# Mixer A's values in two passes, with the sums of the exponentials added up beside them

## The chip, the cores and the metric

The kernel runs on one core of a Trainium2 chip. The metric is the device time of one execution in microseconds. The engines are named as in the profile: PE is TensorE (PEld its weight loads), DVE is VectorE, ACT is ScalarE, POOL is GpSimd, SP issues DMAs.

## The reference

One layer of a hybrid diffusion backbone. 1024 latent tokens and 128 prompt tokens, each 1024 wide, are normed and modulated, projected to queries, keys, values and gates of two mixers (8 heads of 64 over 2 key groups each), attended, gated with SiLU, and projected back. Mixer A attends to all 1024 latent keys and 128 cached ones, mixer B to a window and the cached ones with a sink logit:

```python
def global_attn_latent(q, k_lat, v_lat, k_ctx, v_ctx):      # mixer A
    k_all = jnp.concatenate([k_ctx, k_lat], axis=1)
    v_all = jnp.concatenate([v_ctx, v_lat], axis=1)
    def one_block(qblk):                                    # 128 queries
        s = jnp.einsum('bqkgd,bskd->bkgqs', qblk, k_all).astype(jnp.float32) * (d ** -0.5)
        p = jax.nn.softmax(s, axis=-1).astype(v_all.dtype)
        return jnp.einsum('bkgqs,bskd->bqkgd', p, v_all)
...
def merge_out(o_a, g_a, o_b, g_b, w_out):
    return jnp.concatenate([o_a * jax.nn.silu(g_a), o_b * jax.nn.silu(g_b)], axis=-1) @ w_out
...
xs = xs + gate * merge_out(o_a, g_a, o_b, g_b, w_out[l])
```

All inputs are float32. The outputs are both token sets and the prompt's new keys and values.

## The kernel before

TensorE takes its operands in a rounded 32-bit form (`F32R`). To keep float32 accuracy each operand is kept as a high part (the rounded value) and a low part (what the rounding left), and a product is summed from two or three passes: high x high, and the two mixed ones. Weights, hidden states, keys, values, probabilities (`ph`, `pl`) and gated outputs (`ogh`, `ogl`) are split in this way.

The first 300 us project gates, queries, keys and values. The rest is the attention loop. It goes over `units` (t, m, g): t is a tile of 128 tokens (1 to 8 latent, then 0 the prompt), g the key group with four query heads, m the mixer (0 is A, 1 is B). For a latent t the order is A, B of group 0, A, B of group 1. A unit of mixer A has nine blocks of 128 keys, one of mixer B three or four, a prompt unit one. Each block is a slot of the loop; `tick()` opens a slot and runs what `later(n, f)` put on the agenda n slots before. In each slot the loop issues `scores` for its block, then what is `due`, then some items of the output projection of an earlier tile (2.5 on average), then `values` for the block of three slots before (`LAG`). `in_order` fixes the order of the instructions on each engine to the order in which they are written.

For a block of mixer A, `scores` makes two passes into a PSUM bank "B" (keys by four heads' 128 queries, 512 columns), ScalarE takes the exponential (`pe`), ScalarE rounds it (`ph`), and GpSimd (VectorE for b in `PL_DVE`) subtracts to get `pl`. The maximum that is subtracted in the exponent was found before: `max_items` multiplies the queries with all keys in twelve pieces of 384 columns (`pmx`, bank "A") and VectorE reduces each to its row maximum (`mx`); this is done for the mixer A unit two ahead, spread over slots by `MX_AT`. A later small transposition (`ptm`, also "A") puts the maxima into the queries' low tile `qb`.

`values` accumulates into a bank "C" (`pv`), with 128 rows. The weights `two` are 64 columns of the values' high part beside 64 columns that are 1 for mixer A, and the values' low part for mixer B. So for mixer A rows 64 to 127 hold the sum of the exponentials:

```python
nc.tensor.matmul(pv, two, ph, ...)                  # L1141
if m == 0: nc.tensor.matmul(pv[0:64, :], vl, ph, ...)   # L1143
nc.tensor.matmul(pv, two, pl, ...)                  # L1144
```

After the last block, on the agenda by `END_AT`: `inverse` (for mixer A, ScalarE takes the logarithm of the sums and the exponential of its negative; for B it copies the lower half), `gated` (VectorE multiplies, or adds for B, and GpSimd multiplies with the gate tile `sgl`), `parts` (the split into `ogh`, `ogl`). Once both mixers of a group are done, `out_items` puts 24 passes of the output projection in the queue `outq`. When a tile's projection is complete, VectorE multiplies with the adaLN gate (L1218) and adds the residual (L1219).

Mixer B's softmax works from the other side: `weight_items` computes scores with queries in rows (`sn`, bank "A", slots 0 to 3 of the mixer A unit before), VectorE adds the mask and takes the minimum of the negatives (L942), ScalarE takes the exponential with its sum (L928), and `scores` transposes the result; VectorE makes `pl` from PSUM (L1117). Its inverse sums reach the gate tile through a small DMA, and GpSimd multiplies them into `sgl` (L986).

PSUM has two banks each of "A", "B" and "C", and one each of "D" and "E". `pe` has three buffers (`PES`), `ph` and `pl` four.

Of the kernel before, what the change touches and what calls it, by code (L numbers as in the profile page):

```python
# [9 lines left out]
F32 = mybir.dt.float32  # L10
# [8 lines left out]
P = 128  # L19
D = 1024  # L20
KT = D // P
HD = 64
# [12 lines left out]
KS = (0, 1, 4, 5, 2, 3, 6, 7)  # L35
PL_DVE = (4,)
LAG = 3
# [23 lines left out]
OUTRATE = 2.5  # L61
PADRATE = 3
POOL_LO = ("gb",)
NOG = 5
PES = 3
# [43 lines left out]
def hybrid_step(ctx, tc, x_prompt, x_sample, cache_k_a, cache_v_a, cache_k_b, cache_v_b,  # L109
# [17 lines left out]
    def later(n, f):  # L127

        agenda.setdefault(now[0] + n, []).append(f)
# [577 lines left out]
    v_hi = kv.tile([P, 2, 20, 2, HD], F32R, name="v_hi")  # L707
    v_lo = kv.tile([P, 20, HD], F32R, name="v_lo")

# [369 lines left out]
    ogp = ctx.enter_context(tc.tile_pool(name="ogp", bufs=NOG, side="right"))  # L1079
    w2 = ctx.enter_context(tc.tile_pool(name="w2", bufs=2, side="right"))  # L1080
    def blocks(t, m, g):

        if t == 0:
            k = (khp[:, g, :], klp[0:68, g, :]) if m == 0 else 0
            return [(k, v_hi[:, m, 18 + g], v_lo[:, 18 + g, :])]
        if m == 0:
            return [((kha[:, g, b, :], kla[:, g, b, :]), v_hi[:, 0, 2 * b + g], v_lo[:, 2 * b + g, :]) for b in range(9)]
        p0, p1_ = window(t)
        at = {p: b + 1 for b, p in enumerate(POS)}
        return [(p - p0, v_hi[:, 1, 2 * at.get(p, 0) + g], None) for p in range(p0, p1_)]  # L1090

# [15 lines left out]
    def scores(i, b, blk):  # L1107
# [20 lines left out]
        if b in PL_DVE:  # L1128
            later(1, lambda: nc.vector.tensor_tensor(pl, pe, ph, op=ALU.subtract))
        else:  # L1130
            nc.gpsimd.tensor_tensor(pl, pe, ph, op=ALU.subtract)  # L1131
        return ph, pl

    def values(i, b, last, blk, ph, pl):
        t, m, g = units[i]
        _, vh, vl = blk
        if b == 0:
# [3 lines left out]
        nc.tensor.matmul(pv, two, ph, start=(b == 0), stop=False)  # L1141
        if m == 0:
            nc.tensor.matmul(pv[0:64, :], vl, ph, start=False, stop=False)  # L1143
        nc.tensor.matmul(pv, two, pl, start=False, stop=last)  # L1144
# [5 lines left out]
        def inverse():  # L1150
            v["rs"] = w2.tile([64, 512], F32, tag="rs", name=f"rs{i}", bufs=1)
            if m == 1:
                nc.scalar.copy(v["rs"], pv[64:128, :])
                return
            nc.scalar.activation(v["rs"], pv[64:128, :], AF.Ln)
            nc.scalar.activation(v["rs"], v["rs"], AF.Exp, scale=-1.0)

        def gated():
# [8 lines left out]
            nc.gpsimd.tensor_tensor(of, of, sgl.pop(i), op=ALU.mult)  # L1167
            later(GATE_LATE, lambda: load_gate(i + 2))
            v["of"] = of

# [175 lines left out]
```

## Time and profile before

| | |
|---|---|
| runs | 714.02, 711.7, 713.01; median 713.01 us |
| the profiled execution | 711.52 us, of which the span is 709.6 |
| PE busy | 691.6 us, 97% of the span |
| PEld busy | 558.5 us, 79% |
| DVE busy | 469.3 us, 66% |
| ACT busy | 409.9 us, 58% |
| POOL busy | 334.2 us, 47% |

Busy is the time in which an engine has at least one instruction in work; idle time is given with the instruction that ended it and what it had waited for (the releaser). A group is all instructions of one line, engine and form, with count, summed duration and mean. A matmul's end is modelled, so successive matmuls overlap in the records.

### The profile page before, as it was taken

To read this page: it belongs to the slowest core of one execution; us is meant where nothing else is said; L and a number is where in the kernel's file an instruction comes from. 1 tells how busy PE (TensorE), PEld (TensorE's weight loads), DVE (VectorE), ACT (ScalarE), POOL (GpSimd) and SP (SyncE) were. 2 spreads that over 40 slices of the span, in tenths; PEclk is the share of its full clock that TensorE was granted. 3 is DMA by queue.
4 is the path that set the end of the run, shared out by engine and by line. 5 is a ranking of instruction groups with operands and counts; after the bars stand their busy time and mean duration, and the time that the engine had idled before them with its cause. 6 is when DMAs were issued, how large, how long until landed. Compare 5 with 4: busy or idle time off the path is not lost. (4 is left out here: it accounts for less than half of the span.)

```text
span 709.6 us, 10604 instructions
## 1 busy us (share of the span) xinstructions
PE 691.6 (97%) x3508; PEld 558.5 (79%) x3508; DVE 469.3 (66%) x1019; ACT 409.9 (58%) x829; POOL 334.2 (47%) x356
## 2 busy tenths in 40 slices
PE   7999999999999999989999999999999999999987
PEld 4778988878787889966788888888888888787865
DVE  4667257967848945647867578666775776675662
ACT  5646412412403431188777887787778777877760
POOL 3547023233213421256756655665576557555660
PEclk9999999999999999999999999999999999999999
DMA  8962283358353116332222121212221221222323
GB/s 316 415 211 102 78 302 74 90 154 263 84 139 104 37 39 215 123 108 57 78 68 85 50 82 53 71 57 75 68 82 38 79 71 50 78 72 70 104 67 121
DMA packets 53560, 78.58 MB, mean 111 GB/s; under 512 B 7096, under 2 KB 25720, under 8 KB 52608
## 3 DMA queue, kind: packets, MB, share of 16 engines
q1 hardware_dynamic: 45328, 65.96, 28.1%
q10 hardware_dynamic: 8176, 11.94, 6.3%
q8 instruction: 28, 0.46, 0.3%
q14 instruction: 28, 0.23, 0.1%
HBM read 58.69 MB, written 19.18 MB: 110 GB/s over the span
## 5 line engine op out<-in xcount | busy, mean ns | idle before, releaser
L1131 POOL TENSOR_TENSOR pl<-pe,ph 128x512 fp32r<-128x512 f32 x130 | 167.7, 1292 | 145.0 <-DVE nm L942 67.5
L882 DVE TENSOR_REDUCE mx<-pmx 128x1 f32<-128x384 f32 x192 | 101.4, 552 | 56.3 <-PE pmx L881 54.8
L1123 ACT ACTIVATE pe<-st 128x512 f32<-128x512 f32 x146 | 86.8, 594 | 28.2 <-PE st L1121 27.4
L1127 ACT CAST ph<-pe 128x512 fp32r<-128x512 f32 x146 | 90.6, 621 | 4.8
L1141 PE MATMUL pv<-ph,v_hi 128*128 128x512 f32 x208 | 82.8, 398 | 2.2 <-DVE spare L1165 2.2
L1144 PE MATMUL pv<-pl,v_hi 128*128 128x512 f32 x208 | 82.4, 396 | 0.0
L1212 PE MATMUL po<-wo,ogh 128*128 128x512 f32 x216 | 72.6, 395 | 0.2 <-DVE yt L1219 0.2
L174 POOL TENSOR_TENSOR rs_q<-ms_q,mhalf 128x8 f32<-128x8 f32 x18 | 34.1, 1896 | 80.9 <-DVE ms_q L172 80.9
L942 DVE CUSTOM_DVE_ANT_0 sn<-sn,mask,nsink 128x512 f32<-128x512 f32 (+1 forms) x64 | 46.4, 724 | 38.0 <-PE sn L939 37.6
L881 PE MATMUL pmx<-kha,qt 128*128 128x384 f32 x192 | 61.2, 363 | 0.4 <-ACT pen L928 0.2
L1120 PE MATMUL st<-qt,kha 128*128 128x512 f32 x144 | 58.2, 404 | 1.9 <-ACT pe L1123 1.1
L1121 PE MATMUL st<-qb,kla 68*128 68x512 f32 x144 | 57.5, 399 | 1.1 <-DVE qb L901 1.1
L1143 PE MATMUL pv<-ph,v_lo 128*64 128x512 f32 x146 | 57.6, 395 | 0.0
L1144 PEld LDWEIGHTS pv<-pl,v_hi 128*128 128x128 f32 x208 | 39.2, 189 | 16.4
L928 ACT ACTIVATE pen<-sn,nm 128x512 f32<-128x512 f32 (+2 forms) x72 | 45.0, 626 | 6.5 <-DVE nm L942 3.1
L1116 ACT CAST ph<-st 128x512 fp32r<-128x512 f32 x62 | 36.4, 587 | 19.9 <-PE st L1115 18.7
L1141 PEld LDWEIGHTS pv<-ph,v_hi 128*128 128x128 f32 x208 | 39.3, 189 | 10.6 <-ACT ogh L1177 2.4
L646 ACT CAST qo0q<-ptq 128x512 fp32r<-128x512 f32 x18 | 10.6, 586 | 60.7 <-PE ptq L643 55.8
L1212 PEld LDWEIGHTS po<-wo,ogh 128*128 128x128 f32 x216 | 40.0, 188 | 6.8 <-DVE yt L1219 0.6
L1117 DVE TENSOR_TENSOR pl<-st,ph 128x512 fp32r<-128x512 f32 x62 | 42.5, 686 | 2.7 <-ACT ph L1116 2.1
L1212 PE MATMUL po<-wo,ogl 128*128 128x512 f32 x108 | 42.6, 394 | 0.0
L881 PEld LDWEIGHTS pmx<-kha,qt 128*128 128x128 f32 x192 | 35.6, 191 | 6.4 <-DVE mx L882 1.3
(213 smaller groups left out, 1699.2 us busy)
## 6 DMA issues: line engine op xcount, KB each, us to landing
qt<-qd SPq DMA_DIRECT2D x36, 256.0 KB, 3.0
wm<-in_w_mod_ss_dram SPq DMA_DIRECT2D x7, 1024.0 KB, 10.0
qd<-qo0q ACTq DMA_DIRECT2D x36, 128.0 KB, 2.4
qd<-qo1q ACTq DMA_DIRECT2D x36, 128.0 KB, 2.4
sgl<-gd SPq DMA_DIRECT2D x36, 128.0 KB, 2.2
out_dram<-yt SPq DMA_DIRECT2D x17, 256.0 KB, 2.0
xn<-in_x_sample_dram SPq DMA_DIRECT2D x8, 512.0 KB, 7.2
wg<-in_w_mod_g_dram SPq DMA_DIRECT2D x4, 1024.0 KB, 8.3
```

What stands on the lines that cost most here:

```text
L881: nc.tensor.matmul(pm[:, 0:384], lhs, kha[:, g, 3 * b : 3 * b + 3, :], start=True, stop=True)
L882: nc.vector.tensor_reduce(mx[:, h, b : b + 1], pm[:, 0:384], axis=AX.X, op=ALU.max)
L942: nc.vector.tensor_tensor_reduce(s, s, mask[:, m0 : m0 + n], -1.0, nsink[:, 4 * g + h : 4 * g + h + 1], op0=ALU.add, op1=ALU.min, accum_ou ...
L1120: nc.tensor.matmul(s, kh, qtile[i], start=True, stop=False)
L1121: nc.tensor.matmul(s, kl, qbtile[i], start=False, stop=True)
L1123: nc.scalar.activation(pe, s, AF.Exp)
L1127: nc.scalar.copy(ph, pe)
L1131: nc.gpsimd.tensor_tensor(pl, pe, ph, op=ALU.subtract)
L1141: nc.tensor.matmul(pv, two, ph, start=(b == 0), stop=False)
L1143: nc.tensor.matmul(pv[0:64, :], vl, ph, start=False, stop=False)
L1144: nc.tensor.matmul(pv, two, pl, start=False, stop=last)
L1212: nc.tensor.matmul(po[n], a, wo_parts[KT * n + k][lo], start=(k == KS[0] and p == 0), stop=(k == KS[-1] and p == 2))
```

## The change

For mixer A the values' low part moves into the columns that held ones, as for mixer B, and the pass with `v_lo` goes: `pv` gets high and low products in its two halves from two passes for each block. The sum of the exponentials is made in another way. In a latent unit the nine `pe` are added up in one tile `acc`, by GpSimd for b = 1 to 3 and by VectorE for b = 4 to 8, one slot after the block; `acc` is split into a high part (ScalarE) and a low part (GpSimd) two and three slots after the last addition, and two passes with ones as weights sum both over the keys into a bank "A" five slots after it. A prompt unit, which has one block, passes its `ph` and `pl` to the same two passes. ScalarE takes logarithm and exponential of 256 columns in the layout of the gate tile, GpSimd multiplies the result into `sgl`, and `gated` adds the two halves as for mixer B. `PL_DVE` goes from b = 4 to b = 1, 2, 3; `NOG`, the buffers of `ogh` and `ogl`, from 5 to 4.

```diff
-PL_DVE = (4,)
+PL_DVE = (1, 2, 3)
+SUMS_AT = (2, 3, 5)
+ADDED = 4
-NOG = 5
+NOG = 4
@@ split_values
-        nc.vector.tensor_tensor(v_lo[:, j : j + 2, :], src[:, 0], v_hi[:, 0, j : j + 2, 0, :], op=ALU.subtract)
-        nc.vector.tensor_tensor(v_hi[:, 1, j : j + 2, 1, :], src[:, 1], v_hi[:, 1, j : j + 2, 0, :], op=ALU.subtract)
+        nc.vector.tensor_tensor(v_hi[:, :, j : j + 2, 1, :], src, v_hi[:, :, j : j + 2, 0, :], op=ALU.subtract)
...
-        for b in range(0, 20, 4):
-            later(4 + b // 2, lambda b=b: nc.gpsimd.tensor_scalar(
-                v_hi[:, 0, b : b + 4, 1, :], gain4, 0.0, 1.0, op0=ALU.mult, op1=ALU.add))
+        later(4, lambda: nc.gpsimd.tensor_scalar(ones_v, gain4[:, 0, :], 0.0, 1.0, op0=ALU.mult, op1=ALU.add))
@@ scores
+        if t == 0:
+            later(5, lambda: row_sums(i, ph, pl))
+        else:
+            later(1, lambda: add_up(i, b, pe))
         return ph, pl
+
+    adding, scaling = {}, {}
+
+    def add_up(i, b, pe):
+        if b:
+            (nc.vector if b >= ADDED else nc.gpsimd).tensor_tensor(acc, adding.pop(i), pe, op=ALU.add)
+        adding[i] = acc if b else pe
+        if b < 8:
+            return
+        hi, lo = acc_parts
+        for n, f in zip(SUMS_AT, (lambda: nc.scalar.copy(hi, acc),
+                                  lambda: nc.gpsimd.tensor_tensor(lo, acc, hi, op=ALU.subtract),
+                                  lambda: row_sums(i, hi, lo))):
+            later(n, f)
+
+    def row_sums(i, *parts):
+        ss = bank("A", f"ss{i}")
+        for j, a in enumerate(parts):
+            nc.tensor.matmul(ss[0:HD], ones_v, a, start=(j == 0), stop=(j == 1))
+        iv = w2.tile([P, 2 * P], F32, tag="iv", name=f"iv{i}", bufs=1)
+
+        def inverse():
+            for s in range(2):
+                h = slice(HD * s, HD * s + HD)
+                nc.scalar.activation(iv[h].rearrange("p (c n) -> p c n", c=2),
+                                     ss[0:HD].rearrange("p (c s n) -> p s c n", s=2, n=P)[:, s], AF.Ln)
+            nc.scalar.activation(iv, iv, AF.Exp, scale=-1.0)
+            scaling[i] = iv.rearrange("p (c n) -> p c n", c=2)
+
+        if units[i][0]:
+            later(1, inverse)
+        else:
+            inverse()
@@ values
-        if m == 0:
-            nc.tensor.matmul(pv[0:64, :], vl, ph, start=False, stop=False)
         nc.tensor.matmul(pv, two, pl, start=False, stop=last)
...
-            if m == 1:
-                nc.scalar.copy(v["rs"], pv[64:128, :])
-                return
-            nc.scalar.activation(v["rs"], pv[64:128, :], AF.Ln)
-            nc.scalar.activation(v["rs"], v["rs"], AF.Exp, scale=-1.0)
+            nc.scalar.copy(v["rs"], pv[64:128, :])
...
-                                        op=ALU.add if m else ALU.mult)
-            nc.gpsimd.tensor_tensor(of, of, sgl.pop(i), op=ALU.mult)
+                                        op=ALU.add)
+            v["of"] = of
+            if t and m == 0:
+                later(1, gate_on)
+            else:
+                gate_on()
+
+        def gate_on():
+            if m == 0:
+                nc.gpsimd.tensor_tensor(sgl[i], sgl[i], scaling.pop(i), op=ALU.mult)
+            nc.gpsimd.tensor_tensor(v["of"], v["of"], sgl.pop(i), op=ALU.mult)
             later(GATE_LATE, lambda: load_gate(i + 2))
```

More of the change, by code (lines that the diff above doesn't have):

```diff
@@ L707, in hybrid_step @@
     v_hi = kv.tile([P, 2, 20, 2, HD], F32R, name="v_hi")
-    v_lo = kv.tile([P, 20, HD], F32R, name="v_lo")
+    ones_v = kv.tile([P, HD], F32R, name="ones_v")
     POS = [0, 2, 3, 5, 6, 8, 9, 11]
@@ L1080, in hybrid_step @@
     w2 = ctx.enter_context(tc.tile_pool(name="w2", bufs=2, side="right"))
+    acc = w2.tile([P, 512], F32, name="acc", bufs=1)
+    acc_parts = [w2.tile([P, 512], F32R, name=f"acc{n}", bufs=1) for n in ("h", "l")]
     def blocks(t, m, g):
@@ L1084, in blocks @@
             k = (khp[:, g, :], klp[0:68, g, :]) if m == 0 else 0
-            return [(k, v_hi[:, m, 18 + g], v_lo[:, 18 + g, :])]
+            return [(k, v_hi[:, m, 18 + g])]
         if m == 0:
-            return [((kha[:, g, b, :], kla[:, g, b, :]), v_hi[:, 0, 2 * b + g], v_lo[:, 2 * b + g, :]) for b in range(9)]
+            return [((kha[:, g, b, :], kla[:, g, b, :]), v_hi[:, 0, 2 * b + g]) for b in range(9)]
         p0, p1_ = window(t)
         at = {p: b + 1 for b, p in enumerate(POS)}
-        return [(p - p0, v_hi[:, 1, 2 * at.get(p, 0) + g], None) for p in range(p0, p1_)]
+        return [(p - p0, v_hi[:, 1, 2 * at.get(p, 0) + g]) for p in range(p0, p1_)]
     pvb, og = {}, {}
```

3 lines of the change are left out of this document (1 added, 2 removed).

## The prediction, made before the change was run

> **What bounds the kernel now.** I read the page first (busy shares, the 40 slices, the costliest groups), then busy time by stage, then the order of time of single engines inside one stretch of attention, then the waits.
>
> ```profile
> span 709.6 us, 10604 instructions
> PE 691.6 (97%) x3508; PEld 558.5 (79%) x3508; DVE 469.3 (66%) x1019; ACT 409.9 (58%) x829; POOL 334.2 (47%) x356
> L1131 POOL TENSOR_TENSOR pl<-pe,ph 128x512 fp32r<-128x512 f32 x130 | 167.7, 1292 | 145.0 <-DVE nm L942 67.5
> L1143 PE MATMUL pv<-ph,v_lo 128*64 128x512 f32 x146 | 57.6, 395 | 0.0
> ...
> 320.00:350.00 30.00, 27.73 (x125) 20.60 (x124) 23.79 (x52) 24.70 (x52) 20.75 (x21) 1.00 0.26 75
> 350.00:650.00 300.00, 300.00 (x1450) 241.66 (x1449) 204.69 (x437) 235.17 (x466) 180.06 (x193) 1.00 0.21 65
> ```
>
> The columns of the last two rows are the stretch, its length, then PE, PEld, DVE, ACT and POOL busy, the clock, the DMA share. From 350 to 650 us TensorE never stops (300.00 of 300), at a granted clock of 1.00; VectorE has 68%, ScalarE 78%, GpSimd 60%. So the attention loop is bound by TensorE, and a matmul taken out is worth its pitch, as long as the other engines keep up with a shorter loop. The pitch isn't the 395 ns of the group, since matmuls overlap; it is read from starts:
>
> ```profile
> 493.90 0.40 PE L1141 MATMUL pv<-ph,v_hi 128*128 128x512 f32 x1
> 494.13 0.40 PE L1143 MATMUL pv<-ph,v_lo 128*64 128x512 f32 x1
> 494.37 0.40 PE L1144 MATMUL pv<-pl,v_hi 128*128 128x512 f32 x1
> ...
> 439.85 0.76 DVE L942 CUSTOM_DVE_ANT_0 sn<-sn,mask,nsink 128x512 f32<-128x512 f32 x1 [0.23 <-PE sn L939]
> 463.74 0.76 DVE L942 CUSTOM_DVE_ANT_0 sn<-sn,mask,nsink 128x512 f32<-128x512 f32 x1 [0.24 <-PE sn L939]
> 487.58 0.76 DVE L942 CUSTOM_DVE_ANT_0 sn<-sn,mask,nsink 128x512 f32<-128x512 f32 x1 [0.22 <-PE sn L939]
> ```
>
> 494.37 less 493.90 is two pitches: 0.235 us each. The other three rows are the first mixer B score of three successive pairs of units (one of mixer A with nine key blocks, one of mixer B with about four): the loop turns once in (487.58 - 439.85) / 2 = 23.86 us. Over 300 us that is 12.57 pairs, so a pair holds 204.69 / 12.57 = 16.3 us of VectorE, 18.7 of ScalarE and 14.3 of GpSimd.
>
> **The change part by part, for one pair.**
>
> TensorE: nine `v_lo` passes go, two passes with ones come: -7 x 0.235 = -1.64, leaving 22.2 us. (A prompt unit of mixer A loses one and gains two.) If all of it counted, 16 pairs would give 26 us. The cover over the other engines shrinks by as much.
>
> VectorE: before, one subtraction of the nine `pl` is on it (b = 4); now three are, and five additions (b = 4 to 8). All read two operands in SBUF, as L1129 does. Price by starts:
>
> ```profile
> 473.58 0.69 DVE L1129 TENSOR_TENSOR pl<-pe,ph 128x512 fp32r<-128x512 f32 x1 [1.45 <-ACT ph L1127]
> 474.19 0.55 DVE L882 TENSOR_REDUCE mx<-pmx 128x1 f32<-128x384 f32 x1
> 335.83 3.78 POOL L1131 TENSOR_TENSOR pl<-pe,ph 128x512 fp32r<-128x512 f32 x3
> ```
>
> The next starts 0.61 after L1129: +7 x 0.61 = 4.3, so VectorE works 16.3 + 4.3 = 20.6 us in a pair.
>
> GpSimd: two `pl` less, three additions (b = 1 to 3), the subtraction for the low part of the sum, and one product with the inverse sums. Three in 3.78 us with ends overlapped are 1.25 each; the product is a 128x256 one, some 0.7:
>
> ```profile
> L1167 POOL TENSOR_TENSOR spare<-spare,sgl 128x256 f32<-128x256 f32 x26 | 19.2, 738 | 0.5
> 484.77 0.59 ACT L1155 ACTIVATE rs<-pv 64x512 f32<-64x512 f32 x1 [0.86 <-PE pv L1144]
> 485.39 0.63 ACT L1156 ACTIVATE rs<-rs 64x512 f32<-64x512 f32 x1
> L1177 ACT CAST ogh<-spare 128x256 fp32r<-128x256 f32 x36 | 14.4, 402 | 1.5 <-POOL spare L1167 1.5
> ```
>
> +2 x 1.25 + 0.7 = 3.2, so 17.5 us. ScalarE: the logarithm and exponential on 512 columns go (0.62 + 0.63); in come a plain copy (0.6), the high part of the sum (0.6), and three passes over 256 columns, each near L1177's 0.40: 2.4 - 1.25 = +1.15, 19.9 us. On sums alone every engine still fits under 22.2.
>
> What the sums leave out is that VectorE and GpSimd get in each other's way. The rows that show it lie where `w_out` and the last gate weights are split:
>
> ```profile
> 344.65 1.33 POOL L1131 TENSOR_TENSOR pl<-pe,ph 128x512 fp32r<-128x512 f32 x1 [1.34 <-ACT ph L1127]
> 344.87 1.67 DVE L1038 TENSOR_TENSOR wo_big<-wraw,wo_big 128x512 fp32r<-128x512 f32 x1
> L236 DVE TENSOR_TENSOR wlogb<-rawgb,whigb x4: 691/726/1772, 243.5 to 249.4; 128x512 fp32r<-128x512 f32 x4
> L236 POOL TENSOR_TENSOR wlogb<-rawgb,whigb x4: 1287/1586/1736, 244.4 to 250.1; 128x512 fp32r<-128x512 f32 x4
> L1129 DVE TENSOR_TENSOR pl<-pe,ph x16: 691/693/700, 313.3 to 661.3; 128x512 fp32r<-128x512 f32 x16
> ```
>
> (The last three give shortest / median / longest in ns.) The subtraction at 344.87 takes 1.67 instead of 0.69: GpSimd's subtraction runs until 345.98, and VectorE ends 0.56 after that. It waited 0.98. In L236, where both engines do such subtractions at once, both stretch: 1772 against 691, 1736 against 1287. VectorE's operations with a PSUM operand show no such spread. L1129, the very form that is added eight times, shows none either: 691 to 700 in all 16, because at b = 4 GpSimd waits just then. So the price of a meeting is bounded by 0 (L1129) and 0.98 (L1038). For eight operations in a pair that is 0 to 7.8 us. I take the chance of meeting: GpSimd busy 17.5 of 23.9 = 0.73, the rest of a running operation on average 0.55 (half of 1.25, less for the short ones): 8 x 0.73 x 0.55 = 3.2 us. That is 0.4 for each, just under the middle of the two rows: the additions for b = 4 to 8 are issued in the slots in which GpSimd does five `pl` in a row, unlike L1129's.
>
> The Trainium skill, page "SBUF — State Buffer", section "SBUF: two separate sides", says that one pair of SBUF ports is shared, that a VectorE operation with two SBUF inputs and a GpSimd operation that reads SBUF take it as an exclusive lock, and that the later "fully blocks". L1129's 16 rows alone would say that this form is free of it, and the sum would be rival 1's; by the page each meeting costs all that is left of the other's operation, and the sum is the one below. L1038 and L236 agree with the page.
>
> Waits: VectorE now idles 7.6 us in a pair; the parts of it:
>
> ```profile
> DVE mx L882 <- PE pmx L881: 40.9, 41, 1.5
> DVE sn L942 <- PE sn L939: 34.3, 48, 1.3
> DVE pl L1129 <- ACT ph L1127: 20.3, 14, 2.1
> ```
>
> Over the 15 pairs of this stretch the wait for mixer B's scores is 34.3 / 15 = 2.3 each. These lie in slots 0 to 3, where a score matmul waits for its bank and for TensorE's turn, and don't vanish with more work behind them; the two `pl` for b = 1 and 2 now fall between them and may fill 1.2. I take 1.7, between 1.1 and 2.3. The other waits I let vanish, since VectorE will be late there.
>
> So a pair takes 20.6 + 3.2 + 1.7 = 25.5 us on VectorE, against 22.2 on TensorE: +1.6. How that reaches TensorE: VectorE runs in order, so an addition that waits for GpSimd holds back the row maxima and mixer B's `pl` behind it. The maxima's products, scores, transposes and now the sums share two PSUM banks ("A"); a product can't start until the reduction two before it has read its bank. TensorE stalls there, in slots 5 to 12. In slots 1 and 2 `ss` takes a turn in these banks as well: the next score waits for the logarithms, which stand ahead of the score's exponential on ScalarE. ScalarE is dense there, so `pe` of b = 2 to 4 comes some 1.1 us later, and additions with it; I count that in the 1.7. A `pe` buffer (three) is now held until its addition: two slots of slack, free. The gate loads are issued a slot later on SP, which idles; NOG 4 instead of 5 isn't reached in the steady pairs. The ones and the value splits are in a stage where TensorE is busy without a gap; free.
>
> The sum: 13 steady pairs and the two of t = 1. In the latter TensorE has gaps already (27.73 of 30), so its saving counts for little; I take the same +1.6. 15 x 1.6 = 24.0. In the last pair (t = 8, second group) no nine-block unit follows, the twelve maxima are absent, VectorE is free and TensorE's saving counts: -1.6. The prompt units: two matmuls more (0.5) against two shorter inverses (-0.6 each) where TensorE waits for the bank `pv`: 0. Together +22.4. The profiled execution took 711.52: 733.9. The median of the runs, 713.01, is 1.5 above it: 735.5 us.
>
> **The rivals.**
>
> 1. Additions fall into GpSimd's gaps, as L1129 does: no port cost. VectorE has 20.6 + 1.7 = 22.3, level with TensorE, and order decides:
>
> ```profile
> 455.35 1.02 DVE L882 TENSOR_REDUCE mx<-pmx 128x1 f32<-128x384 f32 x2 [0.96 <-PE pmx L881]
> 477.23 1.02 DVE L882 TENSOR_REDUCE mx<-pmx 128x1 f32<-128x384 f32 x2 [1.27 <-PE pmx L881]
> 478.17 0.69 DVE L1218 TENSOR_TENSOR po<-po,wo_big 128x512 f32<-128x512 f32 x1
> 484.83 0.68 DVE L901 TENSOR_TENSOR qb<-ptm,diag 4x512 fp32r<-4x512 f32 x1 [0.36 <-PE ptm L900]
> ```
>
> In every second pair the output's two operations stand at 478.17, and VectorE has no gap from 477.23 until 0.36 before 484.83. Two additions (1.22) less 0.36 and some 0.3 of slack make this pair 0.55 longer. The other has gaps (0.96 before 455.35) and gains about 0.75 of TensorE's 1.64. 7 x 0.55 - 6 x 0.75 - 1.6 = -2.3: 710.7 us. Against it: GpSimd's added work goes into those gaps.
>
> 2. TensorE stays the bound, VectorE keeps up: 146 passes less 36 is 110 x 0.235 = 25.9: 687 us. For it: the sums of busy time, all under 22.2. Against it: VectorE would have to run at 93% in order without one wait that TensorE feels. It is the other side: it decides from a port cost under 0.5 us in a pair, if the waits for scores close too.
>
> 3. GpSimd never idles when VectorE asks: each of eight waits L1038's 0.98, 7.8 in a pair, while the waits for scores vanish: 28.4, +4.5 x 15 - 1.6 = +66: 779 us. For it: five `pl` in a row behind the three additions. Against it: GpSimd's 17.5 leave it idle a quarter of the time.
>
> **How the numbers follow.** The forecast has 0.64, with a range of its own from 710 to 760 (a port cost of two thirds to four thirds of 3.2, waits of 1.1 to 2.3: -0.1 to +3.3 in a pair). Rival 1 has 0.13, rival 2 0.13, rival 3 0.10. 0.3% (2.1 us) is about what a measurement here can tell from no change. Faster: rival 2 and 0.05 of rival 1, 0.18. Same: 0.05 of rival 1 and 0.02 of the forecast, 0.07. Slower: 0.75. The range of 8 in 10 leaves out rival 2 below and most of rival 3 above: 706 to 758.
>
> **What would show it.** Right: the `pl` on VectorE and the additions with means well over 0.69 and longest near 1.9; GpSimd's `pl` longer than 1.29; TensorE under 95% busy between 350 and 650, its idle time before `pmx`, put down to VectorE's reductions; a pair of 25 to 26 us by the starts of `sn`. `ss` should start without a wait. Wrong: additions at a flat 0.69 (no port cost), or TensorE still at 300 of 300 with pairs of 22.2.

## The result, and the profile after

The changed kernel takes 766.58 us (median of four runs, 766.33 to 769.15) against 712.49 (711.7 to 714.02) before: a ratio of 1.0764, 95% interval 1.0734 to 1.0795. The forecast was 735.5 us, range 706 to 758. The direction is right, the loss is more than twice as large: 54 us instead of 22. The profiled execution took 769.15 us, with a span of 767.4.

The page of the changed kernel: span, engines, and the groups that the prediction named; the last line is `pmx` before the change.

```profile
span 767.4 us, 10712 instructions
PE 707.7 (92%) x3398; PEld 549.5 (72%) x3398; DVE 583.6 (76%) x1121; ACT 425.2 (55%) x881; POOL 423.8 (55%) x402
L1132 POOL TENSOR_TENSOR pl<-pe,ph 128x512 fp32r<-128x512 f32 x98 | 141.4, 1455 | 86.2 <-ACT ph L1128 76.6
L880 PE MATMUL pmx<-kha,qt 128*128 128x384 f32 x192 | 76.3, 414 | 30.3 <-DVE mx L881 28.1
L1143 DVE TENSOR_TENSOR acc<-acc,pe 128x512 f32<-128x512 f32 x80 | 88.2, 1103 | 5.4 <-ACT pe L1124 2.0
L1130 DVE TENSOR_TENSOR pl<-pe,ph 128x512 fp32r<-128x512 f32 x48 | 50.8, 1059 | 15.2 <-ACT ph L1128 14.7
L1143 POOL TENSOR_TENSOR acc<-acc,pe 128x512 f32<-128x512 f32 x32 | 44.6, 1392 | 5.7 <-PE st L1122 4.5
...
L881 PE MATMUL pmx<-kha,qt 128*128 128x384 f32 x192 | 61.2, 363 | 0.4 <-ACT pen L928 0.2
```

110 matmuls went, as planned, and TensorE still shows 16 us more busy time: the records of `pmx`, where it stalls most, went from a mean of 363 ns to 414, and at times the granted clock is lower (below). The additions and subtractions on VectorE take 1103 and 1059 ns instead of 690, GpSimd's subtraction 1455 instead of 1292. TensorE's idle time ahead of `pmx` went from 0.4 us to 30.3, nearly all put down to VectorE's reductions.

Busy time by stretch (length, PE, PEld, DVE, ACT, POOL, clock, DMA share), and what VectorE itself waited for in the same stretch (total, times, longest):

```profile
350.00:700.00 350.00, 320.98 (x1407) 238.67 (x1407) 304.53 (x549) 255.26 (x522) 258.74 (x238) 0.98 0.19 59
...
DVE sn L941 <- ACT pe L1124: 19.2, 11, 1.7
DVE pl L1130 <- ACT ph L1128: 10.4, 13, 1.1
DVE sn L941 <- PE sn L938: 6.2, 15, 1.6
```

The pairs by the starts of `qb`, once a pair: twelve steady pairs lie between the two rows of each kernel (its third and its fifteenth `qb`), before and after.

```profile
341.99 0.68 DVE L901 TENSOR_TENSOR qb<-ptm,diag 4x512 fp32r<-4x512 f32 x1
628.03 0.68 DVE L901 TENSOR_TENSOR qb<-ptm,diag 4x512 fp32r<-4x512 f32 x1 [0.36 <-PE ptm L900]
...
353.12 0.68 DVE L900 TENSOR_TENSOR qb<-ptm,diag 4x512 fp32r<-4x512 f32 x1
675.84 0.68 DVE L900 TENSOR_TENSOR qb<-ptm,diag 4x512 fp32r<-4x512 f32 x1
```

A pair took 286.04 / 12 = 23.84 us and takes 322.72 / 12 = 26.89. Over the 13 pairs of the 350 us, VectorE works 304.53 / 13 = 23.4 us in each and idles 3.5; TensorE is busy for 92% of the time, no longer for all of it.

Where the 57.8 us of span came from, by the starts of `qb`. The first `qb` is made ahead of the loop, so the table begins with the second:

| part | before | after | change | predicted |
|---|---|---|---|---|
| before the second `qb` | 303.4 | 306.0 | +2.7 | 0 |
| first two pairs | 38.6 | 47.1 | +8.5 | +3.2 |
| twelve steady pairs | 286.0 | 322.7 | +36.7 | +19.2 |
| last three stretches between `qb` | 48.7 | 53.2 | +4.5 | 0 |
| after the last `qb` | 32.9 | 38.3 | +5.4 | 0 |

The first row is spread between executions: other kernels below with the same code up to there reach the second `qb` at 302.4 to 306.0, and the median run is 2.6 us shorter than the profiled one. In the prediction's sum one more pair with +1.6 and the last with -1.6 make the 0 of the fourth row.

How an addition loses its time, in order of time of VectorE, GpSimd and the products for the maxima:

```profile
474.26 0.68 DVE L1143 TENSOR_TENSOR acc<-acc,pe 128x512 f32<-128x512 f32 x1
474.74 1.36 POOL L1132 TENSOR_TENSOR pl<-pe,ph 128x512 fp32r<-128x512 f32 x1 [1.42 <-ACT ph L1128]
476.66 2.53 DVE L1143 TENSOR_TENSOR acc<-acc,pe 128x512 f32<-128x512 f32 x2
476.90 1.74 POOL L1132 TENSOR_TENSOR pl<-pe,ph 128x512 fp32r<-128x512 f32 x1
478.60 1.18 POOL L1208 TENSOR_TENSOR spare<-spare,sgl 128x256 f32<-128x256 f32 x1
479.11 1.01 DVE L881 TENSOR_REDUCE mx<-pmx 128x1 f32<-128x384 f32 x2
479.71 0.19 PEld L880 LDWEIGHTS pmx<-kha,qt 128*128 128x128 f32 x1 [0.53 <-DVE mx L881]
```

The addition at 474.26 meets an idle GpSimd until nearly its end and takes 0.68. The two at 476.66 take 2.53 instead of 1.30 (0.61 to the next start and 0.69), among GpSimd's subtraction (1.74 instead of 1.29) and gate product (1.18 instead of 0.73). The two reductions of maxima stand behind them and start at 479.11; the next product of TensorE waits 0.53 for its bank. This is the path that the prediction described.

In every second pair an output tile's two operations stand on VectorE as well, and the stall is longer. The addition behind them, the product that waits, and the windows behind the stall, in two such pairs:

```profile
400.73 1.58 DVE L1143 TENSOR_TENSOR acc<-acc,pe 128x512 f32<-128x512 f32 x1
402.83 0.44 PE L880 MATMUL pmx<-kha,qt 128*128 128x384 f32 x1 [1.96 <-DVE mx L881]
404.00:407.00 3.00, 3.00 (x12) 2.62 (x11) 2.41 (x7) 1.57 (x4) 1.75 (x2) 0.50 0.24 78
...
456.69 0.45 PE L880 MATMUL pmx<-kha,qt 128*128 128x384 f32 x1 [1.95 <-DVE mx L881]
458.00:461.00 3.00, 2.90 (x17) 2.08 (x16) 2.96 (x8) 1.69 (x3) 1.72 (x2) 1.00 0.24 75
```

Six steady pairs hold such a stall of 1.95 to 1.96 us. Behind four of them the granted clock falls to 0.50 for some 3.4 us, and these pairs take 27.8 to 27.9 us; behind two it stays at 1.00, and these take 26.8. So some 4 of the 36.7 us lie in the clock, by this one trace; no run isolates it. Before the change the clock is 1.00 throughout the loop.

### The profile page after: what moved, and what is told of

Same layout as the page of the kernel before. It is cut to its first block, busy times and chain, and to the rows that moved or that the text cites. A ratio compares the mean times of both kernels' runs of the same rounds, so it can differ in the third digit from the quotient of the medians.

```text
span 767.4 us, 10712 instructions
## 1 busy us (share of the span) xinstructions
PE 707.7 (92%) x3398; PEld 549.5 (72%) x3398; DVE 583.6 (76%) x1121; ACT 425.2 (55%) x881; POOL 423.8 (55%) x402
## 4 chain that ended last, share of the span: by engine, by line
PE 52%; DVE 29%; ACT 8%; issue 6%; DMA 2%; POOL 2%; ACTq 1%; DVEq 0%; SPq 0%; POOLq 0%
DVE acc L1143 9%; PE po L1252 6%; DVE mx L881 5%; PE pq L253 4%; PE pq L251 4%; PE pq L252 4%; DVE pl L1130 4%; PE pg L265 3%; PE pg L261 3%; PE pg L266 3%; PE pmx L880 2%; ACT pe L1124 2%; PE pv L1179 2%; ACT ph L1128 2%; PE pv L1180 2%
## 5 line engine op out<-in xcount | busy, mean ns | idle before, releaser
L1132 POOL TENSOR_TENSOR pl<-pe,ph 128x512 fp32r<-128x512 f32 x98 | 141.4, 1455 | 86.2 <-ACT ph L1128 76.6
L881 DVE TENSOR_REDUCE mx<-pmx 128x1 f32<-128x384 f32 x192 | 100.4, 546 | 14.2 <-PE pmx L880 13.7
L880 PE MATMUL pmx<-kha,qt 128*128 128x384 f32 x192 | 76.3, 414 | 30.3 <-DVE mx L881 28.1
L1124 ACT ACTIVATE pe<-st 128x512 f32<-128x512 f32 x146 | 86.6, 593 | 24.5 <-PE st L1122 22.7
L1143 DVE TENSOR_TENSOR acc<-acc,pe 128x512 f32<-128x512 f32 x80 | 88.2, 1103 | 5.4 <-ACT pe L1124 2.0
L1179 PE MATMUL pv<-ph,v_hi 128*128 128x512 f32 x208 | 85.4, 411 | 3.8 <-DVE spare L1197 3.8
L1180 PE MATMUL pv<-pl,v_hi 128*128 128x512 f32 x208 | 84.9, 408 | 1.6 <-POOL pl L1132 1.5
L941 DVE CUSTOM_DVE_ANT_0 sn<-sn,mask,nsink 128x512 f32<-128x512 f32 (+1 forms) x64 | 46.1, 721 | 27.9 <-ACT pe L1124 19.2
L1130 DVE TENSOR_TENSOR pl<-pe,ph 128x512 fp32r<-128x512 f32 x48 | 50.8, 1059 | 15.2 <-ACT ph L1128 14.7
L1117 ACT CAST ph<-st 128x512 fp32r<-128x512 f32 x62 | 36.4, 587 | 24.5 <-PE st L1116 23.6
L1179 PEld LDWEIGHTS pv<-ph,v_hi 128*128 128x128 f32 x208 | 40.9, 197 | 11.9 <-issue 4.8
L1143 POOL TENSOR_TENSOR acc<-acc,pe 128x512 f32<-128x512 f32 x32 | 44.6, 1392 | 5.7 <-PE st L1122 4.5
L1180 PEld LDWEIGHTS pv<-pl,v_hi 128*128 128x128 f32 x208 | 40.9, 197 | 9.4 <-POOL pl L1132 2.6
L648 ACT CAST qo0q<-ptq 128x512 fp32r<-128x512 f32 x18 | 10.6, 587 | 61.7 <-PE ptq L645 59.3
```

The lines of the kernel that those rows point to most:

```text
L880: nc.tensor.matmul(pm[:, 0:384], lhs, kha[:, g, 3 * b : 3 * b + 3, :], start=True, stop=True)
L881: nc.vector.tensor_reduce(mx[:, h, b : b + 1], pm[:, 0:384], axis=AX.X, op=ALU.max)
L1124: nc.scalar.activation(pe, s, AF.Exp)
L1143: (nc.vector if b >= ADDED else nc.gpsimd).tensor_tensor(acc, adding.pop(i), pe, op=ALU.add)
```

## The experiments

Times are medians. The edits are in shorthand: bodies are joined to their line, and `...` stands for what is left out. The kernel before took 711.4 to 712.5 us in each series. In the first four texts P stands for the port as the main cost, W for waits that the order brings whatever the port does, C for the chain that makes the inverse sums: rounding of `acc`, the passes with ones (`ss`), logarithm and exponential (`iv`), product with the gate.

**Two passes alone.** No additions and no chain; mixer A's output isn't divided.

```diff
-PL_DVE = (1, 2, 3)
+PL_DVE = (4,)
...
-        if t == 0: later(5, lambda: row_sums(i, ph, pl))
-        else: later(1, lambda: add_up(i, b, pe))
...
-            if m == 0:
-                nc.gpsimd.tensor_tensor(sgl[i], sgl[i], scaling.pop(i), op=ALU.mult)
```

> The changed kernel without any sums (no additions, no two passes with ones, no inverse; mixer A's output is left undivided) and with PL_DVE back at b = 4. It shows what the two value passes are worth by themselves. Theory P (VectorE's operations with two SBUF inputs and GpSimd's shut each other out; the rest of the change would fit): TensorE is the bound again, 146 passes of 0.235 us less than before, 34 us: about 679 us, TensorE busy without a gap from 350 to 600 us, pairs of 21.7 us. Rival W (no port, VectorE and the in-order waits are at their limit as soon as the loop is shorter): pairs of 22.5 to 23.5 us, 690 to 706 us.

686.87 us, ratio 0.9656 (0.964 to 0.9672); pairs of 22.2 us, between the figures of the two theories. Without the passes with ones 146 matmuls are gone, 34.3 us by their pitch; 24.5 came back, and in a steady pair 1.7 of 2.1. Where the rest went wasn't followed up. So the price of the sums is 766.6 - 686.9 = 79.7 us, and the rest of the study splits it.

**One operand in SBUF.** Eight reductions of `pe` in the place of eight additions, all on VectorE, all subtractions on GpSimd; the chain stays, on a tile that is filled once and of which the reductions write 64 columns, so the sums aren't the true ones.

```diff
+    nc.gpsimd.memset(acc, 1.0)
...
-            (nc.vector if b >= ADDED else nc.gpsimd).tensor_tensor(acc, adding.pop(i), pe, op=ALU.add)
+            nc.vector.tensor_reduce(acc[:, 8 * b : 8 * b + 8], pe.rearrange("p (a d) -> p a d", d=64),
+                                    axis=AX.X, op=ALU.add)
...
-PL_DVE, ADDED = (1, 2, 3), 4
+PL_DVE, ADDED = (), 1
```

> The changed kernel with the same amount of work on each engine but no meetings on the port: all nine pl on GpSimd, and in place of eight additions on VectorE eight reductions over pe of the same 512 columns, which have one SBUF input (so the sums are wrong sums: the additions are left out). VectorE has 8 x 0.6 us added to the kernel before's 16.3 less one pl, the same 20.5 us as in the changed kernel; GpSimd the same 17.5. Theory P: the reductions take a flat 0.68, GpSimd's pl a flat 1.29, a pair takes under 24 us, 706 to 724 us in all. Rival W (time of instructions and in-order waits, not meetings): the same as the changed kernel within 6 us, 760 to 770 us.

**True additions in the same places.** Sums in full.

```diff
-PL_DVE, ADDED = (1, 2, 3), 4
+PL_DVE, ADDED = (), 1
```

> The counterpart of the kernel with reductions: the same split (nine pl on GpSimd, eight operations on VectorE), but true additions with two SBUF inputs. Theory P: additions average 1.0 to 1.15 us, GpSimd's pl 1.4 to 1.5, and the time is that of the changed kernel within 10 us (756 to 776); what it has over the kernel with reductions is the port alone. Rival W: within 6 us of the kernel with reductions.

729.26 us with one operand (ratio 1.0261, 1.0227 to 1.0295), 779.74 with two (1.0954, 1.0938 to 1.0971). The groups, first of the kernel with reductions, then of the one with additions:

```profile
L1144 DVE TENSOR_REDUCE acc<-pe 128x8 f32<-128x512 f32 x128 | 85.9, 679 | 34.0 <-ACT pe L1125 33.1
L1133 POOL TENSOR_TENSOR pl<-pe,ph 128x512 fp32r<-128x512 f32 x146 | 186.4, 1287 | 100.9 <-ACT ph L1129 46.8 <-DVE nm L941 44.4 <-DVE acc L1144 8.4
...
L1143 DVE TENSOR_TENSOR acc<-acc,pe 128x512 f32<-128x512 f32 x112 | 114.4, 1021 | 36.0 <-ACT pe L1124 34.1
L1132 POOL TENSOR_TENSOR pl<-pe,ph 128x512 fp32r<-128x512 f32 x146 | 202.9, 1399 | 103.2 <-ACT ph L1128 50.5 <-DVE nm L941 47.5 <-PE pv L1180 3.9
```

Same engines, same counts, same places; with the second SBUF operand both VectorE's and GpSimd's operations stretch, and 50.5 us are lost: 0.39 for each of 128 additions. That is theory P's part; in it lies a lower clock of TensorE too, 0.96 over the steady pairs with additions against 1.00 with reductions. But the kernel without these meetings is still 18 us slower than before, above P's figure. The port isn't all.

**Additions without the chain.** The changed kernel's additions and subtractions; no rounding, no `ss`, no `iv`, no product, so mixer A's output isn't divided.

```diff
-        if t == 0: later(5, lambda: row_sums(i, ph, pl))
...
-        for n, f in zip(SUMS_AT, (...)): later(n, f)
...
-            if m == 0:
-                nc.gpsimd.tensor_tensor(sgl[i], sgl[i], scaling.pop(i), op=ALU.mult)
```

> The changed kernel with its additions where they are, but without what follows them: no high and low part of the sum, no passes with ones, no logarithm and exponential, no product with the gate tile (the output is left undivided). Theory P: the chain costs little, 1 us in a pair (ScalarE 1.7 us, GpSimd 2.0 us, two passes less): 745 to 758 us. Rival C (the chain through ScalarE and the two banks A makes the waits that the prediction put too low: 1.8 us in a pair and the tail): 715 to 738 us.

752.84 us (1.0573, 1.0536 to 1.061), inside what P expected; beside the additions the chain costs 13.7 us.

**The chain without additions.** `acc` filled once, one subtraction on VectorE as before, the chain in full.

```diff
-PL_DVE = (1, 2, 3)
+PL_DVE = (4,)
...
+    nc.gpsimd.memset(acc, 1.0)
...
-        if b: (nc.vector if b >= ADDED else nc.gpsimd).tensor_tensor(acc, adding.pop(i), pe, op=ALU.add)
-        adding[i] = acc if b else pe
```

> Two passes and the whole chain of the sums (rounding to high and low, the two passes with ones, logarithms, exponential, product with the gate), but no additions: the tile that is summed is filled once, so the output isn't divided by the true sums. One of the nine subtractions is on VectorE, as before the change. Theory S (the chain has a price of its own, about the 14 us that its removal gave beside the additions: a bit in each pair, the rest in the prompt and the tail): 697 to 704 us. Rival L (the chain only costs where VectorE is already late from the additions, so that beside two passes alone it shows in the tail only): 689 to 696.

**Reductions without the chain.** The edit of the reductions and that of the additions without the chain together.

> Eight reductions with one SBUF operand in the place of the additions (as in the kernel with one operand), all nine subtractions on GpSimd, and no chain of the sums; the output isn't divided by the sums. Theory S (the chain costs about 14 us wherever it stands): 713 to 717. Rival W (the chain's cost is hidden behind waits of the eight operations for ScalarE's exponentials, which remain): 721 to 727. Two passes alone took 686.9, so the rest is what eight more operations in order on VectorE cost without any meeting at the port.

The chain alone gives 718.4 us (1.0099, 1.0076 to 1.0122), beyond both theories: 31.5 us over two passes alone, and on its own enough to make the change a loss. The reductions alone give 697.05 (0.98, 0.978 to 0.982), below both theories: 10.2 us, in which one subtraction has moved to GpSimd too. 686.9 + 31.5 + 10.2 = 728.6, and the two together took 729.26. Without the port the parts add up. The additions as they are, without the chain, cost 752.84 - 686.9 = 66 us, the chain alone 31.5; that makes 97.5, and the whole cost 79.7. So 18 us of the chain's price are not added to that of the port. The trace of the kernel with additions and no chain shows one reason. Counted between the third and the fifteenth `qb`, VectorE idles 2.3 us in each pair where the changed kernel has 3.4, but works 24.2 instead of 23.5: its subtractions stretch further (1237 ns instead of 1059). So a pair is only 0.4 shorter.

**Is it the prompt's sums?**

```diff
-        if t == 0: later(5, lambda: row_sums(i, ph, pl))
...
-            if m == 0:
+            if t and m == 0:
                 nc.gpsimd.tensor_tensor(sgl[i], sgl[i], scaling.pop(i), op=ALU.mult)
```

> The changed kernel, but the prompt's units make no sums (no passes with ones, no inverse, no product with the gate; the prompt's mixer A output stays undivided); the latent loop is untouched. Theory T (the prompt's product on GpSimd waits for the inverse sums, holds mixer B's row sums behind it and with them VectorE, and TensorE then stands and runs at a lower granted clock for some us): 5 to 8 us less than the changed kernel, 758 to 762, and no granted clock under 0.9 after 730 us. Rival M (the prompt's sums cost only their own two passes and the low clock in the tail comes anyway): 764 to 767.

765.74 us (1.0753, 1.0735 to 1.0771): no. The stall in the tail stayed, and the trace showed whose it is.

**The last latent unit of mixer A without its chain.**

```diff
-        if b < 8:
+        if b < 8 or i == 30:
             return
...
-            if m == 0:
+            if m == 0 and i != 30:
```

> The changed kernel, but the last latent unit of mixer A (tile 8, second group) makes no sums, so its output stays undivided; the prompt's units keep theirs. Theory T (GpSimd's product with the inverse sums of this unit waits behind the exponentials of the prompt's scores, holds the prompt's row sums on GpSimd, VectorE behind them, and TensorE for some 4 us, after which it runs at a lower clock): 4 to 6 us less than the changed kernel, 760 to 763, with the granted clock over 0.9 after 730 us. Rival M (the tail is late for other reasons): 765 to 768.

761.82 us (1.0702, 1.067 to 1.0733): 4.8 less. In order of time, from the changed kernel: ScalarE, GpSimd, VectorE, TensorE, and the windows.

```profile
734.14 0.42 ACT L1164 ACTIVATE iv<-iv 128x256 f32<-128x256 f32 x1
734.63 0.74 POOL L1207 TENSOR_TENSOR sgl<-sgl,iv 128x256 f32<-128x256 f32 x1 [2.49 <-ACT iv L1164]
736.14 0.20 POOL L973 TENSOR_TENSOR sum<-sum,ex 128x4 f32<-128x4 f32 x1
736.37 0.18 DVE L976 RECIPROCAL inv<-sum 128x4 f32<-128x4 f32 x1 [3.02 <-POOL sum L973]
736.58 1.97 DVE L979 TENSOR_SCALAR pen<-pen,inv 128x128 f32<-128x128 f32 x4
738.48 0.84 DVE L1197 TENSOR_TENSOR spare<-pv,rs 64x256 f32<-64x256 f32 x2
739.46 0.77 PE L1179 MATMUL pv<-ph,v_hi 128*128 128x512 f32 x1 [3.67 <-DVE spare L1197]
743.44 0.63 PE L1179 MATMUL pv<-ph,v_hi 128*128 128x512 f32 x1
743.87 0.63 PE L1180 MATMUL pv<-pl,v_hi 128*128 128x512 f32 x1
...
735.00:740.00 5.00, 1.33 (x5) 0.82 (x4) 2.93 (x8) 3.44 (x9) 3.12 (x5) 0.84 0.09 26
740.00:745.00 5.00, 5.00 (x15) 3.78 (x14) 2.31 (x5) 1.78 (x4) 3.45 (x6) 0.50 0.18 54
```

The unit's inverse sums stand on ScalarE behind the exponentials of the prompt's scores. GpSimd's product waits 2.49 us for them, and the prompt's `sum` stands behind it; VectorE's `inv` waits 3.02 for `sum`, and the addition that frees bank `pv` stands behind that (with L979 stretched to 1.97; it takes 0.88 in the kernel without the chain); TensorE stands still for 3.67 us. Then it runs at a granted clock of 0.50: 743.87 less 743.44 is a pitch of 0.43 us instead of 0.235. Without this unit's chain the clock stays at 1.00 in each 5 us from 725 on. The page "TensorE: Matmul & The Clock Gate" of the Trainium skill, section "Part 1: The HAM clock gate", says that an idle window of about 3.4 us brings the clock down to half; the trace agrees here, with 3.67 us and 0.50. The loop shows it with less than that sentence has: there the clock fell behind stalls of 1.95 us, in four of six cases.

**Where the chain's price lies in the loop: moved, other bank, other reader.** Three slots later, in the changed kernel and in the chain alone (the last tile's units unmoved):

```diff
-        for n, f in zip(SUMS_AT, (
+        for n, f in zip(SUMS_AT if units[i][0] == 8 else SUMS_AT[:2] + (8,), (
...
-                later(1, gate_on)
+                later(1 if t == 8 else 4, gate_on)
...
+        if m == 0 and 0 < t < 8:
+            ends = ends[:2] + (ends[2] + 3,) + ends[3:]
```

> The changed kernel with the passes with ones three slots later (behind the four scores of mixer B rather than among them), the gate's product and the split of mixer A's output three slots later with them; the last tile's two units as in the changed kernel. Same work. Theory A (the sums' turn in the two banks A, whose logarithms stand ahead of the scores' exponentials, delays the scores, and with them VectorE and the blocks behind): 8 to 12 us less, 755 to 759. Rival P (the loop is paced by VectorE's stretched additions, a delay of the scores is only waiting that VectorE has anyway): 764 to 769.

> The kernel with the chain of the sums but no additions (718.4 us), with the two passes of ones three slots later, behind mixer B's four scores (last tile's units unmoved); as there, the output isn't divided by the true sums. Theory A (the chain's price in the loop is its turn in the two banks A, which holds mixer B's scores back while TensorE is the bound): pairs from 23.5 back to 22.4 to 22.7, 12 of them, 705 to 709 us. Rival O (it is the work that the chain puts on the in-order queues of ScalarE and GpSimd, wherever it stands): 715 to 720.

767.63 us in the changed kernel (1.0787, 1.0771 to 1.0803), which is nothing; 733.93 in the chain alone (1.0312, 1.0281 to 1.0343), 15.5 worse and above both ranges. Theory A, the turn in the banks, failed; but the product with the gate and the split moved too, so the next runs take these apart. VectorE's reciprocals in the place of the logarithms and the exponential tell nothing on it:

```diff
-                nc.scalar.activation(iv[h]..., ss[0:HD]..., AF.Ln)
-            nc.scalar.activation(iv, iv, AF.Exp, scale=-1.0)
+                nc.vector.reciprocal(iv[h]..., ss[0:HD]...)
```

> The kernel with the chain but no additions (718.4 us), with VectorE's reciprocals out of PSUM (two, 64x256) in the place of ScalarE's two logarithms and one exponential; the output isn't divided by the true sums. Theory O (the price is ScalarE's order: three passes over 256 columns, 1.2 us, ahead of the scores' exponentials, and mixer A's own exponentials behind them): 12 pairs shorter by 0.6 to 1.0 and some us in the tail, 704 to 712. Rival A (the banks' turn counts, whoever reads it): 715 to 720.

755.42 us (1.0608, 1.0584 to 1.0632). The group of the reciprocals:

```profile
L1160 DVE RECIPROCAL iv<-ss 64x256 f32<-64x256 f32 x36 | 63.0, 1750 | 2.8 <-PE ss L1154 2.3
```

Two of them, 3.5 us in order on VectorE, are a new cost of their own; inconclusive.

With `ss` in a bank of the pair B, the chain alone and the changed kernel:

```diff
-        ss = bank("A", f"ss{i}")
+        ss = bank("B", f"ss{i}")
```

> The kernel with the chain of the sums but no additions (718.4 us; output not divided by the true sums), with the sums' product in a bank of the scores' pair B instead of the pair A. Its 12 steady pairs were 1.4 us longer than with two passes alone: 0.47 are the two passes with ones, about 1 is TensorE waiting for banks A. Theory A (the sums' turn in A itself): 0.5 to 1.0 less in each pair, 704 to 712 us. Rival O (banks A come free late because ScalarE reads them late, whatever bank the sums use): 715 to 720. It could also be slower, if the scores now wait for the logarithms: over 721.

> The changed kernel with the sums' product in a bank of the pair B instead of A; all sums in full. If VectorE's stretched additions pace the loop, the bank is no matter: 764 to 769 us. If the bank's turn counts here too: 752 to 760.

717.84 us (1.0086, 1.0069 to 1.0104) and 765.57 (1.0763, 1.0747 to 1.0779): the other bank gains nothing in either. The next candidate is ScalarE's order. The waits of the chain alone between 350 and 600 us (10.6 pairs), and one place of it:

```profile
PEld pmx L880 <- ACT pen L927: 6.7, 10, 0.7
ACT ogh L1215 <- POOL spare L1206: 5.0, 11, 1.4
PEld sn L937 <- ACT pen L927: 3.9, 11, 0.9
...
473.43 0.73 POOL L1205 TENSOR_TENSOR sgl<-sgl,iv 128x256 f32<-128x256 f32 x1
474.24 0.75 POOL L1206 TENSOR_TENSOR spare<-spare,sgl 128x256 f32<-128x256 f32 x1
475.02 0.41 ACT L1215 CAST ogh<-spare 128x256 fp32r<-128x256 f32 x1 [0.36 <-POOL spare L1206]
475.34 0.68 ACT L927 ACTIVATE pen<-sn,nm 128x512 f32<-128x512 f32 x1
476.16 0.19 PEld L880 LDWEIGHTS pmx<-kha,qt 128*128 128x128 f32 x1 [0.69 <-ACT pen L927]
```

GpSimd makes one product more ahead of the gated output; ScalarE waits for it with the split `ogh`, in order; mixer B's exponential stands behind, and it holds bank A, for which TensorE's next product waits 0.69. In the kernel moved by three slots the wait of `ogh` was 11.1 us instead of 5.0. So the split was put two slots later, alone, with bank B as well, and in the changed kernel:

```diff
+        if t and m == 0:
+            ends = ends[:2] + (ends[2] + 2,) + ends[3:]
```

> The kernel with the chain but no additions (718.4 us; output not divided by the true sums), with the split of mixer A's gated output two slots later, the rest of the chain where it was. In it ScalarE stands in order before that split, waiting for GpSimd's two products (0.36 us and more, in each pair), and mixer B's exponentials, which free banks A, stand behind it. Theory O (this wait is part of the 1 us of TensorE's waits): 0.3 to 0.6 less in each pair, 710 to 715 us. Rival A (only the bank's turn counts): 716 to 720.

> Both edits on the chain without additions: sums in a bank of the pair B, and the split two slots later. If each takes a part of the wait: 700 to 708 us, pairs of 22.5 to 22.9. If neither counts: 715 to 720.

> The changed kernel with the split of mixer A's gated output two slots later (the edit that took 9.2 us from the chain without additions); all sums in full. If the waits of the chain and of the port add up: 755 to 759 us. If VectorE's stretched additions pace the loop, so that the chain's waits lie beside theirs (18 us of overlap by the runs so far): 762 to 768.

709.21 us (0.9962, 0.9949 to 0.9974), 708.73 (0.996, 0.9948 to 0.9973) and 766.39 (1.075, 1.0706 to 1.0794). Theory O holds: the one edit takes 9.2 us off the chain alone, a little more than expected, pairs fall from 23.5 to 23.1, and the wait of `ogh` is gone from the list. With bank B as well nothing more is gained, so neither range for both edits was met. In the changed kernel the edit takes nothing; that the stretched additions pace the loop there, and this wait lies beside them, fits but is argued.

**Additions from PSUM.** Full sums; the exponential of blocks 5 to 8 stays in its bank.

```diff
-        pe = w3.tile([P, 512], F32, tag="pe", name=f"pe{i}_{b}", bufs=PES)
+        far = t and b >= ADDED
+        pe = s if far else w3.tile([P, 512], F32, tag="pe", name=f"pe{i}_{b}", bufs=PES)
...
-        if b in PL_DVE:
+        if far:
...
-ADDED = 4
+ADDED = 5
```

> The changed kernel with the same sums in full, but for the blocks 5 to 8 the exponential stays in its PSUM bank, and VectorE's four subtractions and four additions read it there: one operand in SBUF each instead of two. Counts as in the changed kernel: eight such operations on VectorE, nine on GpSimd. Theory P (the port, met by operations with two SBUF operands, makes most of the loss): 727 to 740, with VectorE's additions at a flat 0.7 and GpSimd's subtractions at 1.29. Rival B (the loss is in the order and the waits; or the two banks B, now held until the addition, stop the scores): 755 or more.

822.44 us (1.1548, 1.1527 to 1.157). The groups:

```profile
L1144 DVE TENSOR_TENSOR acc<-acc,st 128x512 f32<-128x512 f32 x64 | 43.5, 679 | 41.8 <-POOL acc L1144 41.8
L1144 POOL TENSOR_TENSOR acc<-acc,pe 128x512 f32<-128x512 f32 x48 | 61.2, 1276 | 0.0
L1121 PEld LDWEIGHTS st<-qt,kha 128*128 128x128 f32 x144 | 30.8, 214 | 82.6 <-DVE acc L1144 67.9 <-issue 5.8 <-ACT pe L1125 2.3
```

P's signs are there: 679 ns flat on VectorE, 1276 on GpSimd. Yet it is the slowest kernel, by rival B: VectorE's first addition waits for GpSimd's last one, and until then the score's bank is held; TensorE's score weights waited 67.9 us for these additions. Two accumulators might cut this wait; that wasn't tried. These additions depend on one another as those with two SBUF operands do, so the dependence is not what stretches the latter.

No kernel here with full sums comes near the one before. By the parts that add up, additions free of the port (10.2) and the chain with the later split (709.2 - 686.9 = 22.3) would make some 719 us, an estimate, still above 712.

## Why the prediction was right in direction and wrong in size

- **TensorE's passes**: right in count, too high in worth. Two passes alone gave 24.5 us for 34.3; a pair took 22.2 us without the passes with ones, and the prediction's 22.2 has them in it. The forecast went by VectorE, so this moved only rival 2.
- **VectorE's work, +4.3 in a pair, and port, +3.2**: right. The stretch is 80 x (1103 - 690) + 48 x (1059 - 690) ns = 50.7 us, 3.2 for each of 16 pairs; busy time per pair 23.4, forecast 23.8 (20.6 + 3.2). The chance of meeting was an estimate, and it fell out well.
- **"The other waits I let vanish", waits 1.7**: this step failed; it measured 3.5, and 12 pairs at 3.05 instead of 1.6 are 17.5 us of the miss. The waits ahead of the scores' reductions were sized well: (19.2 + 6.2) / 13 = 1.95 us in a pair. The waits taken to vanish did not: VectorE's `pl` kept 10.4 / 13 = 0.8 of the 20.3 / 15 = 1.35 before, and smaller ones make up the rest. By the rows VectorE catches up behind a stall and then waits again. Waits and stretching can't be split sharply, though: without the chain VectorE idles 2.3 and works 24.2, and the pair of 26.5 is still 1.0 above the forecast. Some 4 of the 17.5 us lie in TensorE's half clock, which the prediction, reading 1.00 before, put at nothing.
- **The chain priced by busy time alone** ("on sums alone every engine still fits", "I count that in the 1.7"): wrong. 31.5 us alone, 13.7 beside the additions. What the prediction looked for, the turn of `ss` in banks A with the logarithms, has no price that two runs could find, though in the changed kernel the scores' weight loads waited for these logarithms 14 times, 4.0 us in all. What it didn't look for, ScalarE standing at the split for GpSimd's extra product, costs 9.2 us of the chain alone. Its 32 passes are 7.5. Of the rest, 31.5 - 9.2 - 7.5 = 14.8, some 5 are the tail (37.6 us after the last `qb` with the chain alone, 32.5 with two passes alone); about 10 were not split further, so their cause stays open. In the changed kernel the 13.7 lie mostly at the end: 5.7 behind the last `qb`, 3.3 in the last three stretches, 0.4 in each steady pair.
- **First two pairs, taken as two ordinary ones**: +8.5 instead of +3.2. The kernels with single parts put it on both: 42.8 us with the chain alone, 47.0 with the additions alone, 38.0 with neither. There VectorE and GpSimd also split `w_out`, with two SBUF operands, on top of what a steady pair holds; that this is the reason was not tested. In the changed kernel TensorE's granted clock also falls to 0.50 twice there (312 to 315 and 339 to 342 us), and never before the change.
- **Last pair -1.6, prompt 0**: wrong sign. The stretches at the end gained 4.5 and the tail 5.4. The last unit's chain makes 4.8 of it. The prediction checked the prompt's own sums for cost (0, and the run without them says 0.8) and not whose instructions the last latent unit's product would hold back on GpSimd.
- **Rivals**: 1, no port cost, is ruled out by means of 1103 and 1059 ns. 2 would have been 687, which two passes alone reached only by leaving out the 36 passes with ones too: a coincidence. 3 assumed a larger port cost than there is; its 779 is nearer than the forecast only because other terms grew.
- **What would show it**: all right (means over 1.0 us, the longest 1.77, `pl` on GpSimd at 1.46, TensorE at 92%, waits ahead of `pmx` for VectorE; `ss` starts with 0.2 us of named waits in all), except the pair, 26.9 instead of 25 to 26.

## What to carry to other kernels

Price an added instruction twice: by its busy time, and by what stands behind it on its engine when its input comes late. A chain whose work fitted in every engine's gaps cost 31.5 us alone; 7.5 were its passes, and 9.2 were one split that waited in order. When a loop's bound moves from one engine to another that runs in order, keep that engine's waits in the sum unless a row shows what removes them. For each product that a unit makes after its last block, look at the last unit too: there it stands ahead of other work, and a stall can cost TensorE's clock as well (here 3.67 us in the tail, and 1.95 us in the loop in four of six cases).

## What the runs showed of the hardware

- The second SBUF operand costs both sides. 128 additions on VectorE rose from 679 ns (reductions, one operand) to 1021 and 897, GpSimd's subtractions from 1287 to 1399, 0.39 us of the kernel's time for each addition. With the other operand in PSUM they were 679 again: two that ran wholly beside GpSimd's operations, a subtraction at 462.25 us and an addition at 465.83, took 0.69 each. The page "SBUF — State Buffer" of the Trainium skill, section "SBUF: two separate sides", describes this as one lock for both engines; these rows agree. The flat 16 rows of L1129 before the change are no evidence against it: at most 0.15 us of any of them lies beside an operation of GpSimd.
- Each waits for what is left of the other's operation. An addition begun at 476.66 would end 0.45 us after GpSimd's subtraction starts at 476.90, and that one takes 1.74 instead of 1.29; the second addition ends 0.55 after it. GpSimd's products are stretched too: 1.18 us instead of 0.73 at 478.60.
- VectorE's reciprocal of 64x256 out of PSUM takes 1750 ns; ScalarE's logarithm with the same shape 374, in this group of the changed kernel:

```profile
L1162 ACT ACTIVATE iv<-ss 64x256 f32<-64x256 f32 x36 | 13.5, 374 | 2.2 <-PE ss L1156 2.0
```
- TensorE at rest for 3.67 us came back at half clock for some 5 us, with a pitch of 0.43 us. Stalls of 1.95 to 1.96 us in the loop were followed by some 3.4 us at half clock in four of six cases.
